# Norm weights loaded into a one-row tile and copied into the zeroed tile, with five more products of ones behind the spreading

## The chip, the cores and the metric

The kernel runs on one core of one Trainium2 chip. The metric is device time in microseconds (us) of one execution; lower is better. Before the change the median of three runs is 1128.49 us (1128.32 to 1130.63).

The core has a matrix engine (TensorE, PE in the profile, with PEld for its weight loads), a vector engine (VectorE, DVE), a scalar engine (ScalarE, ACT), a general engine (GpSimd, POOL) and an engine that here only issues transfers (SyncE, SP). Each engine works through its own instructions in order and waits on semaphores for the others. Transfers (DMAs) are issued by an engine, here SP and ACT, and run beside it.

## The reference

One decoder layer is computed for a prompt (16 meta tokens and 512 tokens) and for 8 samples of 8 tokens, with shared weights. Each of its two blocks begins with a norm; the change touches only the first one:

```python
def rmsnorm(x, w):
    xf = x.astype(jnp.float32)
    y = xf * lax.rsqrt(jnp.mean(xf * xf, axis=-1, keepdims=True) + RMS_EPS)
    return (y * w.astype(jnp.float32)).astype(x.dtype)
...
    xn = rmsnorm(x, p['ln_mix_pre'])
    h = xn @ p['w_in']
```

`x` has 592 rows of 1024 elements, and `ln_mix_pre` is one row of 1024 weights, which every row of `x` is multiplied with. The product with `w_in` (1024 by 5640) feeds differential attention, a gated delta rule and two gates; an output projection and a convolutional feed-forward block follow.

## The kernel before

The kernel keeps the normalised `x` transposed on chip, split in a high and a low part (`xhi`, `xlo`) so that three fast products give the precision of one full float32 product; weights are split in the same way (`whi`, `wlo`). After the first norm almost all of the time is such products on TensorE, with copies, splits and norms on the other engines.

The change lies in `embed` and `embedded`, the first stage. `x` is loaded in five tiles of rows (`x`, the first four from the prompt, the fifth with samples and meta tokens), and between them the first weights (`wraw`, `raw`), all on SP's queue. A tile goes through these steps, which are small functions in `embedded`:

- `square(i)`: ACT sums the squares of tile `i` (L485, with a read of the accumulator).
- `root(i)`: DVE scales the sum (L400), POOL raises it to the power -1/2 (L401). The result is `r`.
- `scale(i, g)`: DVE multiplies half `g` (512 columns) of tile `i` with `r` and with the norm weights `lnb[g]` (L496), giving `xs`.
- `turn(i, g, p)`: TensorE transposes that half in four pieces (L437), with the identity matrix from `constants` as the other operand.
- `high(i, g)` and `low(i, g)`: ACT copies the transposed half into `xhi` (L513), DVE subtracts to get `xlo` (L517). `whigh` (ACT, L520) and `wlow` (POOL, L523) do that for the first weights.
- `product`: the three products of the first two pieces of 128 output columns.

For `scale`, the row of norm weights must stand in all 128 partitions. TensorE spreads it: `row` is a tile of 128 by 1024 that is zeroed by DVE (L449) and gets the weights in its first partition by a DMA (L453); `one` is zero except for ones in its first partition. The product of `one` and half of `row` (L289, through the helper `mm`) has the weights in every partition. The two halves go to the PSUM tiles `lnb[0]` and `lnb[1]`. Because `row` is zeroed first, ACT's queue holds the DMA into `row` back until DVE has done it.

Ahead of the spreading, TensorE multiplies a tile of ones (`warm`) with itself `WARM` = 5 times; nothing reads these products, which go into the PSUM tile `ps_s`. Each float32 product, those of ones and the spreading alike, shows as two records in the trace.

The order of the work of PE, ACT, DVE and POOL in this stage is the order in which the calls are written, inside `manual_schedule`. DMAs issued by SP stand in program order too, and one that takes over the completion semaphore of an earlier DMA waits for that one: `raw` for the first DMA of the program, the fifth `x` tile for the third. After this stage a scheduler orders instructions ahead of time.

Of the kernel before, what the change touches and what calls it, by code (L numbers as in the profile page):

```python
# [17 lines left out]
D = 1024  # L18
# [141 lines left out]
WARM = 5  # L160
# [6 lines left out]
class Body:  # L167
# [272 lines left out]
    def embed(self, pool):  # L440
        nc, a = self.nc, self.a
        with ExitStack() as stack:
            psum = self.pool(stack, "psum_e", space=PSUM)
            lnb = [self.t(psum, [128, 512], "lnb", bufs=2) for _ in range(2)]
            warm = self.t(pool, [128, 128], "warm", bufs=1)
            row = self.t(pool, [128, D], "row", bufs=1)
            one = self.t(pool, [128, 128], "one", bufs=1)
            nc.vector.memset(warm, 1.0)
            nc.vector.memset(row, 0.0)  # L449
            nc.vector.memset(one, 0.0)  # L450
            nc.vector.memset(one[0:1], 1.0)
            nc.scalar.dma_start(self.ident, a["constants"][:, 0:128])
            nc.scalar.dma_start(row[0:1], a["ln_mix_pre"])  # L453
            return self.embedded(pool, lnb, row, one, warm)

    def embedded(self, pool, lnb, row, one, warm):
        nc, a = self.nc, self.a
        xs, raws, w = [], [], a["w_in"][0]
        for i in range(5):
            rows = 128 if i < 4 else NTL  # L460
            x = self.t(pool, [128, D], "x", bufs=5)
            if i < 4:
                nc.sync.dma_start(x, a["x_prompt"][0, 128 * i : 128 * i + 128])
            else:
                nc.sync.dma_start(x[0:64], a["x_sample"].rearrange("b t d -> (b t) d"))
                nc.sync.dma_start(x[64:66], a["meta_tokens"][14:16])
                nc.sync.dma_start(x[66:80], a["meta_tokens"][0:14])
            xs.append((x, rows))
            if i == 1:
                raws.append(self.raw_w(w, C_Q))  # L470
            if i == 3:
                raws.append([self.t(pool, [128, 4, 128], "raw", bufs=2) for _ in range(2)])
                for k, raw in zip((0, 512), raws[1]):
                    nc.sync.dma_start(raw, w[k : k + 512, C_Q + 128 : C_Q + 256].rearrange("(k p) c -> p k c", p=128))

        r, y, ps = {}, {}, {}
        whi = [self.t(self.wpool, [128, 8, 128], "whi", F32R, bufs=2) for _ in range(2)]
        wlo = [[self.t(self.wpool, [128, 4, 128], "wlo", F32R, bufs=WLO) for _ in range(2)] for _ in range(2)]
        ws = [([h[:, k] for k in range(8)], [l[k // 4][:, k % 4] for k in range(8)]) for h, l in zip(whi, wlo)]

        def square(i):
            x, rows = xs[i]
            junk = self.t(pool, [128, D], "junk", bufs=1)
            r[i] = self.t(self.small, [128, 1], "ss", bufs=4), self.t(self.small, [128, 1], "r", bufs=4)
            nc.scalar.activation(junk[:rows], x[:rows], AF.Square, accum_out=r[i][0][:rows])  # L485

        def root(i):
            rows = xs[i][1]
            self.rsqrt(r[i][1][:rows], r[i][0][:rows], 1.0 / D, EPS, rows, 1)

        def scale(i, g):
            x, rows = xs[i]
            if not g:
                y[i] = self.t(pool, [128, D], "xs", bufs=5)
            c = slice(512 * g, 512 * g + 512)
            nc.vector.scalar_tensor_tensor(  # L496
                out=y[i][:rows, c], in0=x[:rows, c], scalar=r[i][1][:rows], in1=lnb[g][:rows], op0=ALU.mult, op1=ALU.mult
            )

        def turn(i, g, p):  # L500
            rows = xs[i][1]
            ps[i, g] = p = p.rearrange("p (k c) -> p k c", k=4)
            for k in range(4):
                ch = 128 * (4 * g + k)
                self.transpose(p[:, k, :rows], y[i][:rows, ch : ch + 128])

        def parts(i, g):
            rows = xs[i][1]
            return (e[:, 4 * g : 4 * g + 4] for e in self.part(self.x, (128 * i, 128 * i + rows))), ps[i, g][:, :, :rows]

        def high(i, g):
            (hi, lo), p = parts(i, g)
            nc.scalar.copy(hi, p)  # L513

        def low(i, g):
            (hi, lo), p = parts(i, g)
            nc.vector.tensor_tensor(out=lo, in0=p, in1=hi.bitcast(F32), op=ALU.subtract)  # L517

        def whigh(j, g):
            nc.scalar.copy(whi[j][:, 4 * g : 4 * g + 4], raws[j][g])  # L520

        def wlow(j, g):
            nc.gpsimd.tensor_tensor(  # L523
                out=wlo[j][g], in0=raws[j][g], in1=whi[j][:, 4 * g : 4 * g + 4].bitcast(F32), op=ALU.subtract
            )

        def product(j, c, p, kind, ks, first=False, last=False):
            (hi, lo), (xhi, xlo) = ws[j], self.part(self.x, c)
            for k in ks:
                l, x = {"hh": (hi, xhi), "hl": (hi, xlo), "lh": (lo, xhi)}[kind]  # L530
                self.mm(p, l[k], x[:, k], start=first and k == 0, stop=last and k == 7)

        engines = {mybir.EngineType.PE, mybir.EngineType.Activation, mybir.EngineType.DVE, mybir.EngineType.Pool}
        c0, c1 = HALF_Q
        lower, upper, every = range(4), range(4, 8), range(8)
        with self.tc.manual_schedule(engines=engines):
            p = self.ps("s")[:, :128]
            for _ in range(WARM):
                self.mm(p, warm, warm, start=True, stop=True)
            for g in range(2):  # L540
                self.mm(lnb[g], one, row[:, 512 * g : 512 * g + 512], start=True, stop=True)
            square(0)
            root(0)
            square(1)
            scale(0, 0)
            root(1)
            scale(0, 1)
            whigh(0, 0)
            wlow(0, 0)
            turn(0, 0, self.ps("t"))  # L550
            high(0, 0)
            whigh(0, 1)
            wlow(0, 1)
            scale(1, 0)
            turn(0, 1, self.ps("t"))
            high(0, 1)
            scale(1, 1)
            turn(1, 0, self.ps("t"))
            high(1, 0)
            turn(1, 1, self.ps("s"))  # L560
            high(1, 1)
            for i in range(2):
                for g in range(2):
                    low(i, g)
            square(2)
            root(2)
            square(3)
            p0 = self.psd()[:, : c0[1] - c0[0]]
            product(0, c0, p0, "hh", every, first=True)
            product(0, c0, p0, "lh", every)  # L570
            product(0, c0, p0, "hl", every, last=True)
            scale(2, 0)
            root(3)
            whigh(1, 0)
            whigh(1, 1)
            scale(2, 1)
            p1 = self.psd()[:, : c0[1] - c0[0]]
            product(1, c0, p1, "hh", lower, first=True)
            turn(2, 0, self.ps("t"))
            product(1, c0, p1, "hh", upper)  # L580
            turn(2, 1, self.ps("t"))
            product(1, c0, p1, "hl", every)
            scale(3, 0)
            turn(3, 0, self.ps("t"))
            wlow(1, 0)
            square(4)
            high(2, 0)
            scale(3, 1)
            root(4)
            wlow(1, 1)  # L590
            high(2, 1)
            low(2, 0)
            product(1, c0, p1, "lh", lower)
            turn(3, 1, self.ps("s"))
            low(2, 1)
            high(3, 0)
            high(3, 1)
            scale(4, 0)
            turn(4, 0, lnb[0])
            high(4, 0)  # L600
            scale(4, 1)
            turn(4, 1, lnb[1])
            high(4, 1)
            product(1, c0, p1, "lh", upper, last=True)
            for i in (3, 4):
                for g in range(2):
                    low(i, g)
            p2 = self.ps("t")[:, : c1[1] - c1[0]]
            product(0, c1, p2, "hh", every, first=True)
            product(0, c1, p2, "lh", every)  # L610
            product(0, c1, p2, "hl", every, last=True)
        return [(ws[0], [(p0, c0), (p2, c1)]), (ws[1], [(p1, c0)])]
# [1786 lines left out]
```

## Time and profile before

| | |
|---|---|
| median of three runs | 1128.49 us |
| the profiled execution, its own time | 1128.77 us |
| its span, from first to last instruction | 1127.0 us |
| share of the span in which DVE / ACT / POOL are busy | 65% / 47% / 20% |
| DMA, mean over the span | 139 GB/s |

The times in the profile count from the start of the span. A row of a timeline has the start, the duration, the engine, the line of the kernel, the operation and its tiles, and then in brackets how long the engine had been idle and what ended that. Neighbouring instructions of one kind are merged in a row (x4). A row of groups has the number of instructions, their busy time together and the mean duration of one in ns; on TensorE, whose records overlap, busy time divided by the count is nearer to the spacing of one to the next.

### The profile page before, as it was taken

The numbers are of one execution on the slowest core, as the hardware profiler recorded it, in microseconds if no ns is written. First come the engines' busy times: TensorE is split into PE (matmuls) and PEld (weight loads), VectorE is DVE, ScalarE is ACT, GpSimd is POOL, SyncE is SP. The second block draws the span as 40 slices with busy tenths as digits, with TensorE's granted clock in tenths as the row PEclk, the third lists the DMA queues.
The fourth block names the chain that finished last, engine by engine and source line by source line (L and its number), as shares of the span: only waits on it lengthen the run. The fifth ranks groups of instructions, "written<-read, shape, count | busy, mean of one in ns | idle before, by whom it ended". The sixth has DMA issues, their size and how long they took to land.

```text
span 1127.0 us, 22890 instructions
## 1 busy us (share of the span) xinstructions
PE 1103.0 (98%) x8348; PEld 972.2 (86%) x8348; DVE 730.4 (65%) x1891; ACT 525.3 (47%) x1264; POOL 223.0 (20%) x336
## 2 busy tenths in 40 slices
PE   8999999999999999999999999999999999999997
PEld 6887887787787787799999987899999999988886
DVE  5456667696595467476335665499999999752315
ACT  5244544464464366353334244464555555842311
POOL 3122220120110010010000003334545454300000
PEclk9999999999999999999999999999999999999999
DMA  6376335847756866733234354323333232333213
GB/s 186 89 244 193 101 94 170 273 129 249 254 157 228 291 190 220 240 90 75 57 80 139 93 160 137 116 69 99 103 89 104 87 105 76 115 112 103 85 48 122
DMA packets 167354, 156.93 MB, mean 139 GB/s; under 512 B 12307, under 2 KB 123458, under 8 KB 167241
## 3 DMA queue, kind: packets, MB, share of 16 engines
q1 hardware_dynamic: 162833, 147.08, 42.6%
q0 software_dynamic: 3008, 5.16, 1.6%
q10 hardware_dynamic: 1400, 3.22, 0.9%
q8 instruction: 66, 1.08, 0.4%
q14 instruction: 47, 0.39, 0.1%
HBM read 145.54 MB, written 9.88 MB: 138 GB/s over the span
## 4 chain that ended last, share of the span: by engine, by line
PE 82%; DVE 7%; ACT 3%; issue 3%; DMA 3%; POOL 2%; SPq 0%; DVEq 0%; ACTq 0%; POOLq 0%
PE ps_d L289 31%; PE ps_t L289 20%; PE ps_g L289 15%; PE ps_t L437 7%; PE ps_s L289 7%; PE ps_m L289 1%; DVE wlo L332 1%; ACT KT L1536 1%; DMA wraw<-in_w_out 1%; POOL grr L401 1%; DVE lw L332 1%; DVE cy L770 0%; DVE gf L1860 0%; DMA page<-in_cache_v 0%; DVE fy L2041 0%
## 5 line engine op out<-in xcount | busy, mean ns | idle before, releaser
L289 PE MATMUL ps_d<-xhi,whi 128*128 128x256 f32 (+2 forms) x696 | 213.6, 310 | 0.1
L332 DVE TENSOR_TENSOR wlo<-wraw,whi 128x512 fp32r<-128x512 f32 x190 | 143.3, 772 | 105.3 <-ACT whi L331 103.7
L289 PE MATMUL ps_d<-xhi,wlo 128*128 128x256 f32 (+2 forms) x696 | 208.8, 303 | 1.5 <-DVE wlo L332 1.5
L289 PE MATMUL ps_d<-xlo,whi 128*128 128x256 f32 (+2 forms) x696 | 207.5, 301 | 0.0
L331 ACT CAST whi<-wraw 128x512 fp32r<-128x512 f32 x190 | 113.6, 621 | 166.6 <-PE ps_d L289 73.8
L289 PEld LDWEIGHTS ps_d<-xhi,whi 128*128 128x128 f32 x696 | 130.7, 189 | 6.0 <-issue 3.7
L289 PEld LDWEIGHTS ps_d<-xhi,wlo 128*128 128x128 f32 x696 | 130.3, 189 | 3.7 <-DVE wlo L332 2.0
L289 PEld LDWEIGHTS ps_d<-xlo,whi 128*128 128x128 f32 x696 | 131.0, 190 | 2.1 <-issue 1.8
L1536 ACT COPY KT<-ps_t 128x512 f32<-128x512 f32 x106 | 57.4, 599 | 34.7 <-PE ps_t L437 32.8
L332 DVE TENSOR_TENSOR lw<-sw,hw 128x512 fp32r<-128x512 f32 x76 | 69.7, 918 | 5.3 <-ACT hw L331 5.3
L289 PE MATMUL ps_t<-fhit,hw 128*128 128x290 f32 x228 | 68.3, 300 | 0.9 <-DVE p L2064 0.6
L437 PE MATMUL ps_t<-consts,page 128*128 128x128 f32 x512 | 68.3, 279 | 0.9 <-DMA page<-in_cache_k 0.6
L437 PEld LDWEIGHTS ps_t<-consts,page 128*128 128x128 f32 x512 | 55.6, 140 | 14.6 <-issue 7.7
L289 PE MATMUL ps_t<-fhit,lw 128*128 128x290 f32 x228 | 67.7, 297 | 0.0
L289 PE MATMUL ps_t<-flot,hw 128*128 128x290 f32 x228 | 67.6, 296 | 0.0
L331 ACT CAST hw<-sw 128x512 fp32r<-128x512 f32 x76 | 46.9, 618 | 19.6 <-PE ps_g L289 12.1
L289 PEld LDWEIGHTS ps_t<-fhit,hw 128*128 128x128 f32 x228 | 43.0, 189 | 1.5 <-DVE p L2064 0.8
L289 PEld LDWEIGHTS ps_t<-flot,hw 128*128 128x128 f32 x228 | 43.2, 190 | 0.0
L289 PEld LDWEIGHTS ps_t<-fhit,lw 128*128 128x128 f32 x228 | 43.1, 189 | 0.0
L2039 ACT ACTIVATE fy<-fpre,fw 128x592 f32<-128x592 f32 x22 | 19.5, 885 | 47.6 <-DVE fpre L1999 47.6
L2041 DVE SCALAR_TENSOR_TENSOR fy<-fpre,fw,fy 128x592 f32<-128x592 f32 x44 | 36.5, 829 | 1.0 <-ACT fy L2039 0.4
L1044 POOL DMA_DIRECT2D out_new_gdn_sample<-st x4 | 3.8, 955 | 162.7 <-DVE st L1010 134.3
(721 smaller groups left out, 2888.4 us busy)
## 6 DMA issues: line engine op xcount, KB each, us to landing
page<-in_cache_k SPq DMA_DIRECT2D x128, 256.0 KB, 4.2
page<-in_cache_v SPq DMA_DIRECT2D x128, 256.0 KB, 4.4
wraw<-in_w_in SPq DMA_DIRECT2D x86, 256.0 KB, 3.0
wraw<-in_w_ffn_in SPq DMA_DIRECT2D x50, 256.0 KB, 3.0
wraw<-in_w_down SPq DMA_DIRECT2D x44, 256.0 KB, 2.9
raw<-in_w_ffn_in SPq DMA_DIRECT2D x38, 256.0 KB, 3.0
wraw<-in_w_out SPq DMA_DIRECT2D x16, 256.0 KB, 2.9
x<-in_x_prompt SPq DMA_DIRECT2D x4, 512.0 KB, 7.0
```

The lines of the kernel that those rows point to most:

```text
L289: return self.nc.tensor.matmul(out, lhsT, rhs, **kw).ins
L331: self.nc.scalar.copy(hi, raw)
L332: (eng or self.nc.vector).tensor_tensor(out=lo, in0=raw, in1=hi.bitcast(F32), op=ALU.subtract)
L401: nc.gpsimd.tensor_tensor(out=dst, in0=dst, in1=self.mhalf[:rows, :n], op=ALU.pow)
L437: self.nc.tensor.transpose(out, in_, self.ident[:k, :k])
L1044: nc.gpsimd.dma_start(o["new_gdn_sample"][0, :, h].rearrange("b k v -> k b v"), state)
L1536: copy(kt[:, :, 128 * j : 128 * j + 128], tp)
L2039: nc.scalar.activation(y, pre[:, 0:592], AF.Identity, bias=fw[:, m, 19:20], scale=fw[:, m, 16:17])
L2041: nc.vector.scalar_tensor_tensor(out=y, in0=pre[:, j : j + 592], scalar=fw[:, m, 16 + j : 17 + j], in1=y, op0=ALU.mult, op1=ALU.add)
```

## The change

A new tile `line` (one partition, 1024 elements) gets the norm weights by the first DMA on ACT's queue, and the identity follows as its second. `row` is zeroed as before, and DVE then copies `line` into its first partition in two halves. The two products that spread the row come right behind the copies in the written order. Behind them stand five more products of ones into `ps_s`.

```diff
@@ -443,17 +443,18 @@
             warm = self.t(pool, [128, 128], "warm", bufs=1)
+            line = self.t(pool, [1, D], "line", bufs=1)
             row = self.t(pool, [128, D], "row", bufs=1)
             one = self.t(pool, [128, 128], "one", bufs=1)
+            nc.scalar.dma_start(line, a["ln_mix_pre"])
+            nc.scalar.dma_start(self.ident, a["constants"][:, 0:128])
             nc.vector.memset(warm, 1.0)
             nc.vector.memset(row, 0.0)
             nc.vector.memset(one, 0.0)
             nc.vector.memset(one[0:1], 1.0)
-            nc.scalar.dma_start(self.ident, a["constants"][:, 0:128])
-            nc.scalar.dma_start(row[0:1], a["ln_mix_pre"])
-            return self.embedded(pool, lnb, row, one, warm)
+            return self.embedded(pool, lnb, line, row, one, warm)
...
@@ -538,7 +539,12 @@
             for _ in range(WARM):
                 self.mm(p, warm, warm, start=True, stop=True)
             for g in range(2):
+                c = slice(512 * g, 512 * g + 512)
+                nc.vector.tensor_copy(row[0:1, c], line[:, c])
+            for g in range(2):
                 self.mm(lnb[g], one, row[:, 512 * g : 512 * g + 512], start=True, stop=True)
+            for _ in range(WARM):
+                self.mm(p, warm, warm, start=True, stop=True)
             square(0)
             root(0)
             square(1)
```

On ACT's queue, at the very start of the program, stood:

```order
L452 DMA consts_66<-in_constants 128x128
L453 DMA row_98<-in_ln_mix_pre 1x1024 [waits DVE_49]
L485 ACT_TABLE_LOAD
L485 ACTIVATE junk_142,ss_143<-x_106 128x1024 [waits DMAHW1_49]
L485 ACTIVATE junk_148,ss_149<-x_108 128x1024 [waits DMAHW3_49,Activation_49]
```

And now, at the same place on ACT:

```order
L449 DMA line_98<-in_ln_mix_pre 1x1024
L450 DMA consts_66<-in_constants 128x128
L486 ACT_TABLE_LOAD
L486 ACTIVATE junk_150,ss_151<-x_107 128x1024 [waits DMAHW1_49]
L486 ACTIVATE junk_156,ss_157<-x_109 128x1024 [waits DMAHW3_49,Activation_49]
```

The DMA of the norm weights is now the first and waits for nothing, and no DMA on this queue waits for DVE any more. (`consts` is the tile whose first 128 columns are the identity; DMAHW1 is the semaphore of the first `x` tile.)

On DVE, between the zeroing and the first norm, stood:

```order
L449 MEMSET row_98 128x1024
L450 MEMSET one_99 128x128
L713 MEMSET gc_955 128x40
L451 MEMSET one_99 1x128 [waits DVE_49]
L400 TENSOR_SCALAR r_144<-ss_143 128x1 [waits Activation_49]
L496 SCALAR_TENSOR_TENSOR xs_152<-x_106,r_144,lnb_95 128x512 [waits DMAHW1_49,PE_49,Pool_49]
```

And now, at the same place on DVE:

```order
L452 MEMSET row_99 128x1024
L453 MEMSET one_100 128x128
L719 MEMSET gc_963 128x40
L454 MEMSET one_100 1x128 [waits DVE_49]
L543 COPY row_99<-line_98 1x512 [waits DMAHW0_49]
L543 COPY row_99<-line_98 1x512
L400 TENSOR_SCALAR r_152<-ss_151 128x1 [waits Activation_49]
L497 SCALAR_TENSOR_TENSOR xs_160<-x_107,r_152,lnb_95 128x512 [waits DMAHW1_49,PE_49,Pool_49]
```

Two copies that wait for the DMA into `line` (DMAHW0) now stand ahead of the first root.

On TensorE, from its first product to the second transposed half, stood:

```order
L289 MATMUL ps_s_134<-warm_97 128x128 [waits DVE_49]
L289 MATMUL ps_s_134<-warm_97 128x128 x4
L289 MATMUL lnb_95<-row_98,one_99 128x512 [waits DMAHW2_49,DVE_49]
L289 MATMUL lnb_96<-row_98,one_99 128x512
L437 MATMUL ps_t_159<-consts_66,xs_152 128x128 [waits DMAHW0_49,DVE_49]
L437 MATMUL ps_t_159<-consts_66,xs_152 128x128 x3
L437 MATMUL ps_t_169<-consts_66,xs_152 128x128 [waits DVE_49]
```

And now, at the same place on TensorE:

```order
L289 MATMUL ps_s_135<-warm_97 128x128 [waits DVE_49]
L289 MATMUL ps_s_135<-warm_97 128x128 x4
L289 MATMUL lnb_95<-row_99,one_100 128x512 [waits DVE_49]
L289 MATMUL lnb_96<-row_99,one_100 128x512 [waits DVE_49]
L289 MATMUL ps_s_135<-warm_97 128x128 x5
L437 MATMUL ps_t_167<-consts_66,xs_160 128x128 [waits DMAHW2_49,DVE_49]
L437 MATMUL ps_t_167<-consts_66,xs_160 128x128 x3
```

The spreading waits for DVE's copies in place of a DMA, and the five added products stand between the spreading and the first transpose. Behind these places the order on every engine is the same as before; what SP's queue waits for is the same in name, but the first semaphore (DMAHW0) now belongs to `line` and the third (DMAHW2) to the identity. As the added lines move the numbers below them, L485 to L523 of before are L486 to L524 after.

More of the change, by code (lines that the diff above doesn't have):

```diff
@@ L451, in embed, with embedded @@
             nc.vector.memset(one[0:1], 1.0)
-            nc.scalar.dma_start(self.ident, a["constants"][:, 0:128])
-            nc.scalar.dma_start(row[0:1], a["ln_mix_pre"])
-            return self.embedded(pool, lnb, row, one, warm)
-    def embedded(self, pool, lnb, row, one, warm):
+            return self.embedded(pool, lnb, line, row, one, warm)
+    def embedded(self, pool, lnb, line, row, one, warm):
         nc, a = self.nc, self.a
```

## The prediction

> **What bounds the kernel now.** I read the page first: busy time by engine, then the chain that ended last.
>
> ```profile
> PE 1103.0 (98%) x8348; PEld 972.2 (86%) x8348; DVE 730.4 (65%) x1891; ACT 525.3 (47%) x1264; POOL 223.0 (20%) x336
> PE 82%; DVE 7%; ACT 3%; issue 3%; DMA 3%; POOL 2%; SPq 0%; DVEq 0%; ACTq 0%; POOLq 0%
> ```
>
> TensorE is busy in 98% of the span and makes up 82% of the chain. So an edit is worth what it takes from the 24 us in which TensorE idles, or from work that stands on it alone. Next I asked for busy time by stretch (columns: stretch, its length, then PE, PEld, DVE, ACT, POOL busy with instruction counts, granted clock, DMA share, GB/s).
>
> ```profile
> 0.00:3.60 3.60, 2.49 (x10) 2.21 (x10) 1.49 (x6) 0.91 (x1) 1.97 (x9) 1.00 0.43 142
> 3.60:6.70 3.10, 0.03 (x2) 0.05 (x1) 0.15 (x1) 2.25 (x4) 0.57 (x1) 1.00 1.08 362
> 6.70:10.40 3.70, 3.70 (x6) 1.51 (x7) 0.82 (x3) 0.93 (x3) 0.68 (x2) 1.00 1.07 371
> 10.40:13.90 3.50, 3.00 (x20) 1.94 (x18) 3.50 (x6) 2.87 (x6) 2.40 (x2) 1.00 1.15 254
> 13.90:22.40 8.50, 8.29 (x70) 7.93 (x70) 7.71 (x15) 7.20 (x15) 4.56 (x7) 1.00 0.22 53
> 22.40:42.40 20.00, 20.00 (x147) 19.81 (x145) 8.97 (x40) 6.01 (x17) 0.69 (x4) 1.00 0.56 142
> ```
>
> From 22.4 us TensorE runs without a gap for 20 us. Before that lies the stage of the change, with the longest hole of its kind: 3.1 us from 3.6 to 6.7 in which it does nothing. The chain of waits over this stage names its cause (start, us, what).
>
> ```profile
> 1.22 0.91 DVE row L449
> 2.13 0.03 DVE one L450
> 2.17 4.38 DMA row<-in_ln_mix_pre
> 6.55 0.14 issue
> 6.68 3.68 PE lnb L289 x4
> 10.37 0.02 issue
> 10.39 0.76 DVE xs L496
> ```
>
> The norm weights are loaded after `row` is zeroed; their DMA takes 4.38 us, the spreading 3.68, and only then is the first tile scaled. The timelines of the engines beside it show how much of this another path would hide.
>
> ```profile
> 4.50 1.06 ACT L485 ACTIVATE junk<-x 128x1024 f32<-128x1024 f32 x1 [0.52 <-DMA x<-in_x_prompt]
> 5.68 0.15 DVE L400 TENSOR_SCALAR r<-ss 128x1 f32<-128x1 f32 x1 [3.16 <-ACT junk L485]
> 5.92 0.57 POOL L401 TENSOR_TENSOR r<-r,mhalf 128x1 f32<-128x1 f32 x1 [3.29 <-DVE r L400]
> 8.83 0.75 DVE L496 SCALAR_TENSOR_TENSOR xs<-x,r,lnb 128x512 f32<-128x512 f32 x1 [3.00 <-PE lnb L289]
> 10.83 0.59 ACT L513 CAST xhi<-ps_t 128x512 fp32r<-128x512 f32 x1 [3.19 <-PE ps_t L437]
> 13.27 0.59 ACT L513 CAST xhi<-ps_s 128x512 fp32r<-128x512 f32 x1
> 13.75 1.06 ACT L485 ACTIVATE junk<-x 128x1024 f32<-128x1024 f32 x1
> ```
>
> `r` of the first tile is ready at 6.49 (5.92 + 0.57), but its scaling begins at 8.83, when `lnb[0]` is there. So 2.3 us can go at the first scaling before `x` itself is the limit. From the first `xhi` copy at 10.83 ACT works almost without a pause, through the last copy of the second tile (13.27) and the squares (13.75). I therefore measure the gain at the first `xhi` copy.
>
> **The change, part by part.**
>
> *The load.* Where before `row` waited for the zeroing, `line` is issued first on ACT's queue. Its neighbours for a bound are the identity, which stood there before, and `row` itself.
>
> ```profile
> 0.75 0.42 ACTq L452 DMA_DIRECT2D consts<-in_constants  x1
> 2.17 0.50 ACTq L453 DMA_DIRECT2D row<-in_ln_mix_pre  x1
> 4.70 0.93 SPq L474 DMA_DIRECT2D raw<-in_w_in  x2
> q10 hardware_dynamic: 5, 0.00, 14.5%
> ```
>
> The identity, 64 KB issued at 0.75, had landed by 4.70, where SP's `raw` was waiting for it. The last row, of the DMA view from 2.2 to 2.4, holds the first five packets of ACT's queue, the identity's. `line` is one packet at the head of that queue, so it should move about then. At the least it lands at about 2.5, just behind its packet; at the most as late as `row` did, 4.38 us after issue, at 5.1. I take 3.0, near the packet, since `row` had to queue behind two tiles of `x` and weights that SP had issued by then, and `line` has only the first tile beside it. The identity moves back by one issue (0.42), to some 5.1, and the first transpose needs it far later. SP's `raw` and fifth `x` tile, which wait for the first and third DMA, are issued earlier; ACT takes that tile at 17.0, so nothing waits for them.
>
> *The copies.* No copy of one partition by 512 stands in the trace. The nearest are these:
>
> ```profile
> L973 DVE COPY grhs<-vn 16x128 f32<-16x128 f32 x4 | 0.9, 218 | 0.1
> L900 DVE COPY kn<-ps_t 128x512 f32<-128x512 f32 x4 | 2.7, 677 | 0.0
> ```
>
> That bounds one copy by 0.22 (fewer columns) and 0.68 us (as many, read from PSUM). I take 0.35, nearer to the first, which also reads from SBUF. DVE is free from 2.52 to 5.68, so the copies cost no other engine anything if `line` lands by about 4.5. The first ends at about 3.4, the second at 3.75.
>
> *The spreading and the clock.* The products of ones end at 3.61, so the spreading starts behind them at about 3.6 instead of 6.68. How long it takes depends on TensorE's speed, which changes in this stage:
>
> ```profile
> 1.11 2.50 PE L289 MATMUL ps_s<-warm 128*128 128x128 f32 x10 [1.11 <-DVE warm L448]
> L289 PE MATMUL lnb<-row,one 128*128 128x512 f32 x4 | 3.7, 1070 | 3.1 <-DMA row<-in_ln_mix_pre 3.1
> L289 PE MATMUL ps_t<-v,aT 128*128 128x128 f32 x80 | 11.9, 280 | 0.0
> L289 PE MATMUL ps_g<-lm,kn 64*128 64x512 f32 x16 | 8.2, 622 | 0.0
> 9.63 0.18 PEld L437 LDWEIGHTS ps_t<-consts,xs 128*128 128x128 f32 x1 [0.78 <-DVE xs L496]
> L437 PEld LDWEIGHTS ps_t<-consts,xs x24: 138/140/182, 9.6 to 19.8; 128*128 128x128 f32 x24
> ```
>
> A record of 128 columns takes 0.25 us at the start (2.50/10) and 0.149 later (11.9/80); one of 512 columns 0.92 (3.7/4) against 0.51 (8.2/16). The granted clock reads 1.00 in all stretches, yet the work is slower here by 1.7 to 1.8 times. The last two rows date the change: the first weight load of the transposes at 9.63 still takes 0.18 us, the 23 others 0.14. So TensorE became fast between 9.63 and 10.19, some 3.5 us after the spreading had begun at 6.68; the 2.5 us of products from 1.11 had not been enough. If 3.5 us of unbroken work is what it takes, and the spreading follows without a gap, it becomes fast at 1.11 + 3.5 = 4.6. Then the first record takes 0.92 (to 4.5), the other three 0.51 each: the spreading ends at 6.05. `lnb[0]` is ready at about 5.1, before `r` (6.49).
>
> [...]
>
> *The five products.* Ten records of 0.149 take 1.5 us, so TensorE is through at 7.55. The scaling of the first half now runs from 6.53 to 7.28. The first transposes would start at 7.33 without the added products and start at 7.55 with them, so these cost 0.2 here; their whole price is 2.5 us where they run slowly and block. Four transposes take 0.66 (next row), and the first `xhi` copy begins at about 8.25 instead of 10.83: 2.58 us earlier.
>
> ```profile
> 11.19 0.66 PE ps_t L437 x4
> ```
>
> *What is late next.* DVE's chain: the second root behind the first scaling (about 8.1 on POOL), then three scalings of 0.7 with the last done at 9.75 instead of 12.45. ACT then needs 0.48 to 0.57 per copy, as before. It binds, so the shift carries through to the squares and from there to the unbroken stretch at 22.4. The `x` tiles and weights for it land in time, as ACT waited for none of them from 10.83 on.
>
> The sum: 2.58 us, 2.6 rounded, off the profiled execution's own time of 1128.77 (span 1127.0), or 1126.2. That execution lies 0.28 above the median of the runs shown; counted from the median 1128.49, the forecast is **1125.9 us**, 0.23% less.
>
> **The rivals.**
>
> 1. *The clock rises later.* If the small pause between the products of ones and the spreading restarts the 3.5 us, TensorE is fast at 7.1, when the spreading has nearly run slowly: it ends at 3.6 + 3.7 = 7.3, the five at 8.8, the first copy starts at 9.45, and the gain is 1.4. If it stays slow through the five as well, they end at 9.8, the copy starts at about 10.4, gain 0.4. Times from the median 1127.1 and 1128.1, with 1127.0 as a middle case. For it: the jump before came only after the second start of work. Against: a gap of a tenth need not count.
>
> 2. *Slower: the five products stand in the way.* If `line` lands only at 5.1, as `row`'s 4.38 us would have it, the copies end at 5.5, the spreading runs from 5.6 to 9.3, and the five slow products to 11.8; the first transposes wait for them, the copy starts at 12.5, and the last copy of the second tile, 2.3 later by ACT's own pace, at 14.8 instead of 13.27. That is 1.5 us slower, 1130.0. It decides when the five end later than about 10.3, which at the slow rate means a spreading that begins after 4.1 (10.3 - 2.5 - 3.7). Against it: the packets of ACT's queue at 2.2 to 2.4.
>
> 3. *It does not carry through.* The stage ends earlier, but the gain is taken back by a later wait: 1128.5. Against it, three of the later stretches:
>
> ```profile
> 42.40:60.00 17.60, 17.27 (x167) 14.68 (x166) 8.11 (x34) 5.67 (x13) 6.25 (x7) 1.00 0.18 49
> 60.00:130.00 70.00, 68.28 (x545) 56.32 (x545) 43.70 (x171) 31.75 (x84) 17.00 (x36) 1.00 0.58 183
> 400.00:800.00 400.00, 396.35 (x2990) 362.55 (x2987) 257.99 (x606) 182.94 (x434) 63.04 (x76) 1.00 0.42 123
> ```
>
> TensorE's idle time there is 0.3, 1.7 and 3.7 us, in short waits on work that itself follows TensorE, so hardly anything holds to a fixed time.
>
> **How the numbers follow.** The forecast (gain 2.3 to 3.2) has a chance of 0.54, the late clock 0.30, the gain taken back 0.10, the five in the way 0.06. A measurement of this kernel can tell 0.2% from no change, which is 2.26 us, to 1126.2. All of the forecast's case lies beyond that; the late clock and the lost gain count as no change, so faster is 0.54, same 0.40, slower 0.06. The range goes from 1125.1 (the largest gain, 2.8 at the first copy, with half a microsecond to spare in what follows) to 1128.0 (the late clock but for its worst end). It leaves out the lost gain and the slower case, 0.16. The forecast alone spans 1125.3 to 1126.2.
>
> **What would show it right or wrong.** In the changed profile: DVE's two copies at 3.0 to 3.8, 0.35 us each; the spreading starting within 0.2 us of 3.6 and ending at about 6; the five added products with ten records in about 1.5 us; the first `xhi` copy at 8.25 and the last of the second tile at about 10.7 instead of 13.27; and the unbroken stretch starting at about 19.8 instead of 22.4, with the same distance at the end. Spreading records of 0.9 us throughout, or ten added records in 2.5 us, mean the late clock. Copies at 5 us or later, and transposes that wait for TensorE rather than for DVE, mean the slower case. An early stage with the old end means that the gain was lost behind it.

## The result, and the profile after

| | before | after |
|---|---|---|
| median of 22 runs each | 1129.08 us | 1127.33 us |
| lowest run | 1127.99 us | 1125.84 us |
| the profiled execution, its own time | 1128.77 us | 1128.04 us |
| its span | 1127.0 us | 1126.3 us |

The ratio is 0.9985, with an interval of 0.9978 to 0.9991: 1.75 us less, where 2.6 was forecast. The two profiled executions are only 0.73 apart; that of before lies below its median and that of after above, so the traces tell where time went, and the runs how much. Two of the 22 runs of before, of 1326.93 and 4758.58 us, stand far outside the rest and do not move its median. The page of after, its engines and the chain's shares:

```profile
PE 1104.8 (98%) x8358; PEld 975.1 (87%) x8358; DVE 731.9 (65%) x1893; ACT 524.3 (47%) x1264; POOL 224.5 (20%) x336
PE 80%; DVE 8%; ACT 3%; issue 3%; DMA 3%; POOL 2%; SPq 0%; DVEq 0%; ACTq 0%; POOLq 0%
```

TensorE has ten products and ten weight loads more (five float32 products of two records each), DVE two copies. Busy time by stretch (columns as in the prediction) shows the hole from 3.6 to 6.7 us filled:

```profile
0.00:3.60 3.60, 2.49 (x11) 2.49 (x12) 2.10 (x8) 1.28 (x1) 2.19 (x9) 1.00 0.50 167
3.60:6.70 3.10, 3.10 (x8) 1.31 (x7) 0.69 (x2) 1.88 (x3) 0.57 (x1) 1.00 1.05 338
```

The timelines of the same trace, by engine:

```profile
0.75 0.52 ACTq L449 DMA_DIRECT2D line<-in_ln_mix_pre  x1
2.44 0.68 DVE L543 COPY row<-line 1x512 f32<-1x512 f32 x2
3.40 3.23 PE L289 MATMUL lnb<-row,one 128*128 128x512 f32 x4
4.14 1.06 ACT L486 ACTIVATE junk<-x 128x1024 f32<-128x1024 f32 x1 [1.14 <-DMA x<-in_x_prompt]
6.16 0.75 DVE L497 SCALAR_TENSOR_TENSOR xs<-x,r,lnb 128x512 f32<-128x512 f32 x1 [0.68 <-POOL r L401]
8.22 0.59 ACT L514 CAST xhi<-ps_t 128x512 fp32r<-128x512 f32 x1 [0.59 <-PE ps_t L437]
10.19 0.59 ACT L514 CAST xhi<-ps_s 128x512 fp32r<-128x512 f32 x1
```

The copies begin with no idle time of DVE in front, so `line` had landed by 2.44. The first scaling waits for `r` now and not for `lnb`. The first `xhi` copy stands at 8.22 instead of 10.83, the last of the second tile at 10.19 instead of 13.27. The chain shows the way there, and the start of the next long run of products:

```profile
1.11 2.50 PE ps_s L289 x10
3.61 3.02 PE lnb L289 x4
6.63 1.11 PE ps_s L289 x10
7.75 0.45 PE ps_t L437 x4
8.20 0.02 issue
8.22 0.59 ACT xhi L514
...
19.49 3.56 PE ps_t L289 x24
```

In the chain of before the same piece stood here, so the stage is done 2.98 us earlier:

```profile
22.47 3.56 PE ps_t L289 x24
```

Yet the span is only 0.7 shorter. The first piece of the chain near 600 us after which the distance is gone is this; of before, then of after:

```profile
594.71 6.49 PE ps_d L289 x48
602.92 2.94 DMA wraw<-in_w_out
607.26 3.02 DMA wraw<-in_w_out
612.68 3.05 DMA wraw<-in_w_out
617.58 16.39 PE ps_d L289 x120
```

```profile
592.43 6.49 PE ps_d L289 x48
600.64 4.80 DMA wraw<-in_w_out
606.85 2.97 DMA wraw<-in_w_out
612.21 3.10 DMA wraw<-in_w_out
617.16 16.49 PE ps_d L289 x120
```

The same products start 2.28 us earlier on the left of the loads (594.71 against 592.43) and 0.42 earlier on the right (617.58 against 617.16). The first load, 256 KB that the chain waits for, takes 4.80 instead of 2.94, which is the 1.86 that went. The page's list of DMA issues has the same two numbers as its median from issue to landing; before, then after:

```profile
wraw<-in_w_out SPq DMA_DIRECT2D x16, 256.0 KB, 2.9
```

```profile
wraw<-in_w_out SPq DMA_DIRECT2D x16, 256.0 KB, 4.8
```

That median names 16 loads but stands on one: of these 16, the first load above is the only one to which the trace can put a landing, and in the same chain of after the next two take 2.97 and 3.10.

What else moves on the DMA engines there? In the DMA view (packets, MB, share of the engines), the stretch of 600 to 602 us of after has a packet of the queue that the view calls instruction; in before there is none from 600 to 604, and the next one lies in 604 to 606. After, then before:

```profile
q8 instruction: 1, 0.02, 5.6%
```

```profile
q8 instruction: 1, 0.02, 3.2%
```

The page counts 66 packets of this queue in either kernel:

```profile
q8 instruction: 66, 1.08, 0.4%
```

That is 16 KB each. TensorE's 2 x 8348 records over these 66 are 253 to a packet, an estimate that counts every packet as TensorE's. Below, such a packet is called a fetch, as in the expectations. Whether it has to do with the long load is what the experiments ask.

### The profile page after: what moved, and what is told of

Same layout as the page of the kernel before. It is cut to its first block, busy times and chain, and to the rows that moved or that the text cites. A ratio compares the mean times of both kernels' runs of the same rounds, so it can differ in the third digit from the quotient of the medians.

```text
span 1126.3 us, 22911 instructions
## 1 busy us (share of the span) xinstructions
PE 1104.8 (98%) x8358; PEld 975.1 (87%) x8358; DVE 731.9 (65%) x1893; ACT 524.3 (47%) x1264; POOL 224.5 (20%) x336
## 4 chain that ended last, share of the span: by engine, by line
PE 80%; DVE 8%; ACT 3%; issue 3%; DMA 3%; POOL 2%; SPq 0%; DVEq 0%; ACTq 0%; POOLq 0%
PE ps_d L289 30%; PE ps_t L289 20%; PE ps_g L289 15%; PE ps_s L289 7%; PE ps_t L437 6%; PE ps_m L289 1%; DVE wlo L332 1%; DMA wraw<-in_w_out 1%; DVE cy L776 1%; ACT KT L1542 1%; POOL grr L401 1%; DMA wraw<-in_w_ffn_in 1%; DVE gf L1866 0%; DMA page<-in_cache_v 0%; DVE fy L2047 0%
```

## The experiments

The theory, which took the form given here as the groups came in (each expectation below was written ahead of its own group). **The fetch:** the five products behind the spreading bring 20 more TensorE instructions (10 products, 10 weight loads), so every later fetch comes earlier relative to the work, and one now falls into the first `w_out` load near 600 us. **Rival, scatter:** that load is slow for a reason of its own, from one execution to the next. **Rival, the early stage:** an earlier stage in itself makes the loads collide, the five have no part in it. Each group of kernels ran beside the kernel before on the same chip; ratios are to that one.

**Both kernels again, unchanged.**

> The kernel before, unchanged, to learn its spread and its own clock windows. [...] In its trace the first w_out load of the last branch stretch (at 602.9 before) takes 2.9 us again if the 4.8 us of the changed kernel belong to the change.

> The changed kernel again. The first stage ends 3.0 us earlier again (unbroken stretch from 19.5). If the load of w_out at 600.6 is slow (4.8 us against 2.9) for a reason that lies in the program, such as an instruction fetch at the same place, it is slow again; if it was chance, it takes 2.9 and the end lies nearer to 3 us ahead. Ratio 0.9985 again, 0.9978 to 0.9991.

Before gave 1129.29 us (ratio 0.9994, 0.9985 to 1.0003), after 1127.04 (0.9976, 0.9966 to 0.9986). The gain is there again and larger, 2.6 us on the medians of this group (1129.67 - 1127.04). The first `w_out` load, by the page's number, took 3.1 in before and again 4.8 in after, so scatter would have to strike one kernel only. The stage ended 2.67 earlier this time (19.80), and a window of half clock (0.50 from 49.82 to 53.22) is there in this trace of before (last section).

**The change without the five products.** It ran twice, in two groups.

```diff
                 self.mm(lnb[g], one, row[:, 512 * g : 512 * g + 512], start=True, stop=True)
-            for _ in range(WARM):
-                self.mm(p, warm, warm, start=True, stop=True)
             square(0)
```

> The change without the five products behind the spreading. If they only fill time (the second tile's last copy is held by DVE's scalings), that copy still starts at 10.2 and the time is that of the changed kernel within 0.3 us. If they are needed to keep the clock up, the clock falls or rises later, transposes take 0.22 us instead of 0.165, and the stage ends 0.5 to 2 us later. If they stand in the way, it ends 0.5 us earlier.

> The change without the five products behind the spreading, once more. If TensorE's instruction count before the w_out loads decides whether an instruction fetch falls into the first of them, the load takes 2.9 to 3.1 us here, as before, the lead at 640 us is still 2.3 us or more, and the median lies 0.5 to 2 us under that of the changed kernel in the same call. If the slow load is chance, it is as often slow as there.

The first gave 1126.64 us (0.9975, 0.9963 to 0.9987), the second 1126.04 (0.9973, 0.9964 to 0.9982), the lowest median of all. In the stage nothing is missed: without the five the first four transposes take 0.66, as in the row of before that the prediction shows, and the long run of products starts at 19.74 and 19.18, beside 19.49 in after. In the second one's timelines the first `xhi` copy comes earlier, and the last of the second tile at about the same time as in after:

```profile
7.61 0.59 ACT L514 CAST xhi<-ps_t 128x512 fp32r<-128x512 f32 x1 [0.20 <-PE ps_t L437]
9.98 0.59 ACT L514 CAST xhi<-ps_s 128x512 fp32r<-128x512 f32 x1
```

Its chain near 600 us has the short load, though the work starts earlier still than in after. That speaks against the rival of the early stage:

```profile
592.04 6.49 PE ps_d L289 x48
600.26 2.88 DMA wraw<-in_w_out
604.54 3.01 DMA wraw<-in_w_out
609.95 3.22 DMA wraw<-in_w_out
615.02 16.28 PE ps_d L289 x120
```

Against before it leads by 2.67 ahead of the loads and by 2.56 behind them.

**After once more, in the group of the second run without the five.**

> The changed kernel, third profile, beside the one without the five. By the fetch theory the first w_out load takes 4.8 us again (600.6), and the lead falls from 2.3 to 0.4 us there. By the chance theory it may as well take 2.9.

1127.32 us (0.9984, 0.9975 to 0.9993), 1.28 above the kernel without the five beside it. Run by run the two hardly overlap: of 11 each, 10 without the five are at or below 1126.64 and 10 with them at or above 1126.85. Its chain again has the long load, and a long third one:

```profile
591.63 6.49 PE ps_d L289 x48
599.85 4.43 DMA wraw<-in_w_out
...
611.04 4.16 DMA wraw<-in_w_out
617.04 16.25 PE ps_d L289 x120
```

**The five alone, in the kernel before.**

```diff
             for g in range(2):
                 self.mm(lnb[g], one, row[:, 512 * g : 512 * g + 512], start=True, stop=True)
+            for _ in range(WARM):
+                self.mm(p, warm, warm, start=True, stop=True)
             square(0)
```

> The kernel before with the five products behind the spreading, and the load as it was. The spreading ends at 10.4 as before and the five stand ahead of the first transpose: at the fast rate they add about 1.2 us to the stage, at the slow rate 2.5. If only the early load brings the gain, this is slower than before by 1 to 2 us (ratio 1.001 to 1.002); if the five bring something by themselves, it is not.

1131.07 us (1.0014, 1.0005 to 1.0023): 1.4 more than before on the medians. The chain shows two costs. In the stage the five run slowly and the transposes wait for them:

```profile
6.25 3.75 PE lnb L289 x4
10.00 2.08 PE ps_s L289 x10
12.07 0.45 PE ps_t L437 x4
```

The unbroken run of products starts 1.26 later than in before. Near 600 us the long load is there although this stage is later, not earlier, which settles it against that rival:

```profile
603.88 4.46 DMA wraw<-in_w_out
```

**The five moved ahead, or the ones ahead left out.** The first kernel has ten products of ones ahead of the spreading and none behind, the second none ahead and five behind.

```diff
-            for _ in range(WARM):
+            for _ in range(2 * WARM):
                 self.mm(p, warm, warm, start=True, stop=True)
 ...
-            for _ in range(WARM):
-                self.mm(p, warm, warm, start=True, stop=True)
             square(0)
```

```diff
-            for _ in range(WARM):
-                self.mm(p, warm, warm, start=True, stop=True)
             for g in range(2):
                 c = slice(512 * g, 512 * g + 512)
```

> Ten products of ones ahead of the spreading and none behind: as many TensorE instructions as the changed kernel, in another place. By the fetch theory the first w_out load is slow (4.5 to 4.8 us) as in the changed kernel; if it is the place behind the spreading that matters, it takes 2.9. The spreading starts at 6.1 (3.6 + 2.5) and by then or soon runs at the fast rate, so the first xhi copy starts at about 8.9 and the stage ends 0.3 to 0.8 us later than in the changed kernel.

> No products of ones ahead, five behind the spreading: as many TensorE instructions as the kernel before and the one without the five. By the fetch theory the first w_out load takes 2.9 us. The spreading starts at about 3.1 with the clock low; it becomes fast some 3.5 us later (6.6), so the spreading ends at 6.6 and the five at about 8.2: the stage ends within 0.5 us of the changed kernel.

Ten ahead gave 1128.21 us (0.9990, 0.9978 to 1.0001), none ahead 1127.15 (0.9983, 0.9973 to 0.9992). The first load near 600 us took 4.32 with ten ahead and 3.14 with none ahead, as the count of TensorE's records has it (8358 and 8348) and not the place of the five. But the times do not follow the load alone: none ahead has the short load and is still 1.1 above the kernel without the five in the same group. With ten ahead a part is found elsewhere: its lead over before was 3.17 at the end of the stage and 0.83 ahead of the loads, and most of that went near 182 us, where this trace has a window of half the clock (0.50 from 181.67 to 185.09). In the stage, none ahead came as expected (spreading from 3.07, run of products at 19.54), ten ahead did not: the spreading began at 4.90, not 6.1, the first `xhi` copy came at 7.62, not 8.9, and the stage ended 0.2 earlier than in after, not later.

**More products still.** If it is a matter of where the fetch falls, further products should move it out of the load again.

```diff
-            for _ in range(WARM):
+            for _ in range(2 * WARM):
                 self.mm(p, warm, warm, start=True, stop=True)
```

The first kernel doubles the products ahead of the spreading, the second those behind it too. Each ran once.

> Ten products of ones ahead and five behind, ten more than before. Five more moved the fetch from 2.2 to 1.2 us after the issue of the first w_out load; ten more should move it to about 0.2 to 0.3 after it, mostly ahead of the load's own packets. By the fetch theory the load is then nearly as quick as before (2.9 to 3.6 us); if more TensorE instructions as such make it slow, it takes 4.4 or more.

> Ten products of ones ahead and ten behind, fifteen more than before. By the fetch theory the fetch comes 0.7 us ahead of the issue of the load and is done when its packets move: 2.9 to 3.1 us, as before. If the number of TensorE instructions as such makes it slow, 4.4 us or more. The stage ends 0.6 us or so later for the added products.

They took 1126.84 and 1127.38 us, beside 1129.29 for before. With ten and five the load still took 4.14, a miss: the fetch now began 0.15 us behind the load's release, still inside it. With ten and ten it was out, further than said (1.78 ahead of the release instead of 0.7), and the stage ended 2.0 later than in after, not 0.6:

```profile
593.50 6.49 PE ps_d L289 x48
601.71 3.24 DMA wraw<-in_w_out
606.35 2.98 DMA wraw<-in_w_out
611.73 3.69 DMA wraw<-in_w_out
617.27 16.23 PE ps_d L289 x120
```

**All together.** The fetch's start is that of its 16 KB packet in the trace, counted from the moment when the chain lets the load go. The leads are against the profiled execution of before, at the piece of 6.49 us ahead of the loads, at that behind them, and at a run of 24 products that stood at 781.16 in before. The second column counts records.

| kernel | TensorE products | fetch after release, us | load, us | lead ahead | lead behind | lead at 781 |
|---|---|---|---|---|---|---|
| before | 8348 | 2.18 | 2.94 | 0 | 0 | 0 |
| without the five, second | 8348 | 2.19 | 2.88 | 2.67 | 2.56 | 2.80 |
| none ahead, five behind | 8348 | 2.35 | 3.14 | 1.85 | 1.61 | 1.22 |
| after | 8358 | 1.24 | 4.80 | 2.28 | 0.42 | 0.77 |
| after, again (first group) | 8358 | 1.15 | 4.80 | 2.39 | 0.29 | 1.04 |
| after, again (second group) | 8358 | 1.41 | 4.43 | 3.08 | 0.54 | 1.45 |
| ten ahead, none behind | 8358 | 1.05 | 4.32 | 0.83 | -0.85 | 0.25 |
| five alone in before | 8358 | 1.04 | 4.46 | -0.96 | -2.84 | -1.70 |
| ten and five | 8368 | 0.15 | 4.14 | 2.95 | 0.64 | 1.98 |
| ten and ten | 8378 | -1.78 | 3.24 | 1.21 | 0.31 | 1.44 |

Ten products more, with their weight loads, bring the fetch forward by about 1 us each time (2.2, 1.0 to 1.4, 0.15), then by two. Where it begins while the load is under way, from 0.15 to 1.4 us behind the release, the load takes 4.1 to 4.8; where it comes near the load's end or ahead of it, 2.9 to 3.2. Each of the six traces with the long load loses 1.7 to 2.5 us of lead across the stretch; the other two of the changed ones with 8348 lose 0.1 and 0.3, and so does the first kernel without the five (2.44 ahead, 2.18 behind). That one and the second trace of before are not in the table, since their chains do not stand on the load; there too the fetch begins 2.2 behind its issue, and it takes 2.9 and 3.1.

In after it is the load's end that is late. From 3.0 to 4.0 us behind the release, SP's queue still moves 23 packets, 0.01 MB, in after and none in before; they take 7.6% of the engines' time, about one engine of the 16. That the fetch holds up packets of the load behind it on one engine is the author's reading and not shown: which engine a packet took is not in the trace.

A part of the loss comes back: at 781 us the six traces have regained 0.35 to 1.34 of it. TensorE waits there for work of ACT and DVE, and where it had waited long for the load, it waits less: from 755 to 785 us, 0.9 in before and in the second without the five, 0.5 in after, 0.3 with the five alone, nothing with ten and five. From the column ahead to that at 781 the six traces lose 0.6 to 1.6.

Three things stay beside this. Ten and ten lost 0.9 although its first load was short (its third took 3.69). The third load of 4.16, in the second group's trace of after, is long with no fetch from 3 us ahead of its release to 5 behind it, so fetches are not all that goes with a long load, and not all of the loss is theirs. And the same kernel before, profiled again, stood 0.5 to 0.8 later at the first two places and level at the end, so leads are good to some 0.8 us.

## Why the prediction was right, and where it was not

The measured 1127.33 lies in the stated range, in part by luck: the forecast's own span ended at 1126.2, and the range reached 1128.0 only for a late clock. What took the missing part of the gain was mainly something else.

- **The load and the copies: right, a little early.** `line` was there by 2.44, earlier even than the low bound of 2.5; 3.0 had been taken. The copies took 0.34 each against 0.35.
- **The spreading and the clock: between forecast and first rival.** It started behind the products of ones as said (3.61 in the chain), but ended at 6.63, not 6.05 or 7.3. Other executions of the same kernel had it end between 6.3 and 7.0 (2.88 to 3.62 us long). So neither 3.5 us from the first product nor a fresh start behind the pause fits. The reading that 3.5 us of work is what it takes came from one trace: in the second trace of before the first four transposes, 3.75 us behind the start of the spreading, were still slow (0.87 at 10.12). The moment moves from run to run. (The 1127.0 that the first rival calls a middle case does not lie between its 1127.1 and 1128.1, and two copies that begin at 5.1 would end at 5.8, not 5.5, in the second; nothing hangs on either.)
- **The five in the stage: near enough.** They took 1.11 us, not 1.5, and ended at 7.75 against 7.55. That the first `xhi` copy still came at 8.22, forecast 8.25, has a second cause: the transposes took 0.45 instead of 0.66. Against the kernel without the five, whose first copy came at 7.61 in both traces, they cost 0.3 to 1.0 there (7.87, 8.22 and 8.62 in the three traces of after), and between nothing and 0.6 at the last copy of the second tile (9.89, 10.19 and 10.58 against 9.98 and 10.02). 0.2 was said. At the end of the stage no cost is left that stands out of the scatter (19.31 to 19.80 against 19.18 and 19.74).
- **The stage as a whole: right, a little more.** 2.58 was forecast, 2.98 came (2.67 and 3.16 in the other two traces of after). 2.61 of it is there at the first `xhi` copy; the rest comes behind it, where ACT takes 1.97 instead of 2.44 to the last copy of the second tile, since DVE's three other scalings, which in before waited for the second half of the spreading until 10.39, begin at 7.22. The unbroken run of products started at 19.49, forecast 19.8.
- **"Nothing waits for the fifth tile": not so in every execution.** In before ACT takes that `x` tile at 17.02. In after it takes it at 14.17 without a wait, but in the second group's trace of after it waits 0.25 for it, in the first kernel without the five 0.56 (14.43). So this tile is about the next limit of the stage. The identity, which the tile's DMA waits for, landed at 5.89 in the first group's trace of after, not at some 5.1.
- **"What is late next": carried through within the stage, not to the end.** This is where the forecast failed. The step read TensorE's idle time in the later stretches and found only short waits on work that follows TensorE. Near 600 us such a wait was on a `w_out` load, which does follow; but its length was taken for fixed, and with the five products it was longer. The third rival, "it does not carry through", had the right outcome for a part of the gain, without this mechanism.
- **The mis-sized term is the price of the five products.** The sum has 0.2 us for them, counted in the stage alone. In the three traces of after 1.9 to 2.5 us are lost near 600 us, where the fetch falls into the load, and 1.35 to 1.63 are still missing at 781. The medians show 0.4 (1127.04 against 1126.64) and 1.28 (1127.32 against 1126.04); the first cannot be told from nothing. The second's two intervals against before overlap a little, but the runs of the two kernels hardly do. Without them the medians lie 3.0 and 3.3 below before's, about the 2.7 and 3.3 by which their stages ended earlier. With them it is 1.75, 2.6 and 2.1 in three groups.
- **The slower rival did not come about**, since `line` was early. Its mechanism did in the experiment that put the five alone into the kernel before: ten slow records in 2.08 us, and transposes that waited for them.

Shown by the traces: that the fetch's place goes with TensorE's number of instructions (2.2 to 2.4 us behind the release with 8348 records, 1.0 to 1.4 with 8358, 0.15 with 8368, 1.78 ahead of it with 8378), and that in all twelve the first load is long (4.1 to 4.8) just where the fetch starts in its first half. That the fetch itself delays the load is argued from this and from the late packets. Not settled: in how many executions it does so, since most kernels have one or two traces. The kernel with none ahead is also unexplained in part, with a short load but a gain of 2.2 only.

## What to carry to other kernels

The five products took 1.11 us in the stage, and what went with them showed near 600 us: in the five traces with their ten records more a fetch began 1.0 to 1.4 us behind the release of a load that the chain waits for, instead of 2.2 to 2.4, and the load took 4.3 to 4.8 us instead of 2.9 to 3.1. So when instructions are added, compare the loads on the two chains, not only the stage that was edited; the page's landing times point to them, but one of them can stand on a single load, as here. Filler products are worth keeping only where the trace shows that the work behind them slows down without them; here the version without the five, 1126.04 us at a ratio of 0.9973, has the best ratio of all that ran. A gain early in a long chain should be followed through the chain as a lead over the same instruction of before, since the place where the lead drops shows where to look for its taker; follow it to the end, as a later wait can give a part back (here 0.35 to 1.34 us by 781).

## What the runs showed of the hardware that was not expected

The first `w_out` load near 600 us, 256 KB, took 4.1 to 4.8 us in the six traces where a fetch of 16 KB began in its first 1.4 us, and 2.9 to 3.2 in the other six, though all 66 fetches together take 0.4% of the DMA engines' time over the span.

The row of norm weights, 4 KB, landed sooner where it was issued ahead of the others: it took 4.38 us in before, issued at 2.17, and at most 1.7 in after, issued at 0.75 (2.44 - 0.75).

TensorE was granted half its clock (0.50) for 3.4 us near 50 us in after and in the second trace of before, and with ten ahead near 182 us. In after (stretches as above, the clock is the third number from the end):

```profile
43.66:47.07 3.41, 3.41 (x38) 2.94 (x31) 1.41 (x6) 0.00 (x0) 0.35 (x2) 1.00 0.27 75
47.07:50.48 3.41, 3.41 (x19) 3.41 (x18) 0.53 (x3) 1.94 (x4) 2.90 (x1) 0.50 0.00 0
50.48:53.89 3.41, 3.41 (x24) 3.41 (x24) 2.28 (x14) 0.48 (x2) 0.65 (x1) 1.00 0.00 0
```

The stretch ahead of it has no idle time of TensorE either, with 38 records in its 3.41 us. The same work in the profiled execution of before ran at full clock:

```profile
50.05:53.46 3.41, 3.41 (x29) 3.41 (x28) 0.53 (x3) 1.93 (x4) 2.90 (x1) 1.00 0.00 0
```

It fits 29 products in, where 19 fit at half clock. In after this cost 1.5 us of lead at first: the first product of 336 columns behind it starts at 50.58, against 52.05 in before, 1.47 earlier where 2.98 had been. By 66 us the lead was 2.5 again. Since both kernels have it in some executions, it is no part of the change; it adds to the scatter of single times.
